# A two-block network on one core: inverse roots of the second block as powers on GpSimd, low parts of its weights and the delta rule's gating on VectorE

## The chip, the core and the metric

The kernel runs on one core of one Trainium2 chip. Its time is that of one execution in device microseconds; three executions of the kernel before were timed, and one more was taken with the hardware profiler. TensorE is called PE, VectorE DVE, ScalarE ACT, GpSimd POOL, as the profile calls them; SP is the engine that issues most DMAs.

## The reference, cut to what matters

A sequence of 256 positions of width 1024 passes two transformer blocks in float32. The change touches the second one only, from its mixer on. What it computes there, cut down:

```
h    = rms_norm(x, norm_mix)
qkv, z, a_g, b_g, c_q, c_kv, k_idx, w_idx, ug = split(h @ w_in)
# gated delta rule, 4 heads of 128, on silu(conv4(qkv))
q, k = q * rsqrt(sum(q*q) + eps), k * rsqrt(sum(k*k) + eps)
o    = delta_rule(q, k, v, decay, beta)
y_a  = o * rsqrt(mean(o*o) + eps) * gdn_norm * silu(z)
# attention over the 64 best keys of an index score; q and k are rms-normed
y_b  = sparse_attention(rms_norm(c_q @ w_qb), rms_norm(k of c_kv), v of c_kv, index score)
# convolution of 31 taps, then layer norm and silu
y_c  = silu(layer_norm(conv31(u * sigmoid(gate))))
x    = x + concat(y_a, y_b, y_c) @ w_out
x    = x + cross_attention(rms_norm(x), memory)     # q and k rms-normed per head of 128
x    = x + square(relu(rms_norm(x) @ w1)) @ w2
```

## The kernel before

A float32 matrix product is made of three products of numbers in a reduced format (`fp32r`): a matrix is split into a high part and a low part, and high x high, low x high and high x low are summed in PSUM (`mm3`, lines L232 to L234, and `add_T`, L395 to L397). Activations lie transposed, eight tiles of 128 channels by 256 positions, as `thi` and `tlo`. Weights come by DMA in pieces of 128 x 1024 (`load_w`): `wr` is the raw piece, ACT copies it to `wh` (L220 or L227), and the low part `wl` is `wr - wh`. By a share that `give` sets for each stage, `load_w` hands that subtraction either to POOL in one piece (L228) or to DVE in two halves (L222):

```
self.due += self.share
pool = self.due >= 1
```

In the second block's mixer (`block2_mix`, share `G2`) every fourth weight goes to POOL, in the cross attention (`block2_xa`, share `GX`) four of five, in the last feed-forward (`mlp`, share `GP`) none.

The mixer interleaves its parts by generators: `gdn_decay` and `tri_inverse` (the decay matrices `gam`, the key products `nqs`, and a triangular inverse in six doubling levels of two matrix products, a transpose and an addition, L1382 to L1389 and L1367) and then `gdn` lead; `fill2` fills in between with the remaining projections (`rest2`, matmuls into `fl`), the sparse attention (`dsa`) and the convolution of 31 taps on DVE (`conv31`, `cv_y`, L1514), at the end `conv_norm` and the first half of the output projection (`add_T`). A program then orders the instructions of each engine before the kernel runs; each engine executes its own list in that order and waits, in order, on semaphores. The lists are those shown below. `conv_silu` writes the four-tap convolutions `kq` and `vT`: ACT writes the first tap (L1070), DVE adds three (L1072).

Inverse roots are of two kinds. `rms_pow` sends a power of -0.5 to POOL as one instruction (L284). `rsqrt` computes a first guess from the bits and two Newton steps in seven (one column) or nine small instructions on DVE (L250 to L260). The second block calls `rsqrt` for `dsk` and `dsq` (keys and queries of the sparse attention, 2 and 8 columns), `gdr` twice (lengths of the delta rule's keys and queries, 8 columns), `rms` twice in `conv_norm`, `gdo` for each of the two chunks in `gdn` (4 columns), `xaq` twice in `block2_xa` (4 columns) and `raw` in `mlp`.

At the end of `gdn`, for each chunk of 128 positions, ACT sums the squares of the four heads, POOL multiplies the output by `silu(z)` (L1341), DVE multiplies by the root (L1343), and PE transposes the product (L1346) for the second half of the output projection. In the cross attention the row maxima `nm` are scaled by the root `xaq_y` (L892) before ACT's exponential.

Of the kernel before, what the change touches and what calls it, by code (L numbers as in the profile page):

```python
# [8 lines left out]
F32 = mybir.dt.float32  # L9
# [4 lines left out]
ALU = mybir.AluOpType  # L14
AX = mybir.AxisListType
PSUM = bass.MemoryType.PSUM

FW0 = 1
R1, R2, DS, CV, CK, CV0, NW, FW, WARM, WARM2, G1, GM, GF, G2, GX, GP = 2.0, 2.5, 3, 0.5, 1, 0.25, 24, 14, 7, 4, 0.05, 0.2, 0, 0.25, 0.8, 0
T = dict(bp=0, bq='gpsimd', xq='scalar', cp=3, w=(2,3,7,8), n=32, hold=1)  # L20
P = 128
SCRATCH = 4096
S = 256
D = 1024
NEG = -1.0e30
EPS = 1e-6
GDN_SCALE = 128 ** -0.5
# [90 lines left out]
class Net:  # L118
    def __init__(self, ctx, tc, ins, out, dumps=None):
        self.tc, self.nc, self.i, self.out = tc, tc.nc, ins, out  # L120
        self.dumps = dumps or {}
        pool = lambda n, b=1, **k: ctx.enter_context(tc.tile_pool(name=n, bufs=b, **k))
        self.cp = pool("cp")
        self.wp = pool("wp", 4)
        self.ap = pool("ap")
        self.sp = pool("sp", 2)
        self.pp = pool("pp", 4, space=PSUM)
        self.dp = pool("dp", 1, space=bass.MemoryType.DRAM)
        self.n = 0
        self.con = self.gate = None  # L130

    def give(self, share):

# [22 lines left out]
    def constants(self):  # L156
        nc = self.nc
        self.con = self.cp.tile([P, NCON], F32, tag="con", name="con")
        self.col = self.cp.tile([P, NCOL], F32, tag="col", name="col")
        self.srow = self.cp.tile([P, NSROW], F32, tag="srow", name="srow")  # L160
        n = CON["upper"]
        nc.scalar.dma_start(self.con[:, :n], self.i["const"][:, :n])
        n = COL["mix_norm_pre"] + NCH
        nc.scalar.dma_start(self.col[:, :n], self.i["cols"][:, :n])
        self.ident = self.con[:, CON["ident"]:CON["ident"] + P]
        self.upper = self.con[:, CON["upper"]:CON["upper"] + P]
        self.ones = self.cp.tile([P, P], F32, tag="ones", name="ones")
        nc.gpsimd.memset(self.ones, 1.0)
        self.mhalf = self.cp.tile([P, 1], F32, tag="mhalf", name="mhalf")
        nc.gpsimd.memset(self.mhalf, -0.5)  # L170
        self.zero = self.cp.tile([1, 512], BF16, tag="zero", name="zero")
        nc.gpsimd.memset(self.zero, 0.0)
        nc.scalar.activation(self.zero[:, 0:1], self.zero[:, 1:2], AF.Square)
# [68 lines left out]
    def rsqrt(self, v, shape, tag, bufs=2):  # L242


        nc = self.nc
        steps = (-0.703952253, 1.6819141), (-0.5, 1.5000004)
        y = self.t(shape, tag + "_y", bufs=bufs)
        t = self.t(shape, tag + "_t", bufs=bufs)
        h = [self.t(shape, tag + f"_h{k}", bufs=bufs) for k in range(2)]
        nc.vector.tensor_scalar(y.bitcast(I32), v.bitcast(I32), -0.5, 1595932665.0, op0=ALU.mult, op1=ALU.add)  # L250
        for k in range(2):
            nc.vector.tensor_scalar(h[k], v, steps[k][0], None, op0=ALU.mult)
        for k in range(2):
            if shape[1:] == [1]:
                nc.vector.tensor_scalar(t, y, y, h[k], op0=ALU.mult, op1=ALU.mult)
                nc.vector.tensor_scalar(y, t, steps[k][1], y, op0=ALU.add, op1=ALU.mult)
            else:
                nc.vector.tensor_tensor(t, y, y, op=ALU.mult)
                nc.vector.tensor_tensor(t, t, h[k], op=ALU.mult)
                nc.vector.scalar_tensor_tensor(y, t, steps[k][1], y, op0=ALU.add, op1=ALU.mult)  # L260
        return y
# [17 lines left out]
    def rms_pow(self, ss):  # L279

        v = self.t([P, 1], "rms_v", bufs=4)
        self.nc.vector.tensor_reduce(out=v, in_=ss, axis=AX.X, op=ALU.add)
        y = self.t([P, 1], "rms_y", bufs=4)
        self.nc.gpsimd.tensor_tensor(y, v, self.mhalf, op=ALU.pow)  # L284
        return y

    def new_T(self, place=None):
# [1005 lines left out]
    def gdn(self, kq, z, mixT):  # L1293
        nc = self.nc
        H = 4
        edec, ld, dd, kn, gam, nqs, room = self.gd
        inv, os, ws = room[:, 0], room[:, 1], room[:, 2]
        b4 = lambda c: c.unsqueeze(2).to_broadcast([P, H, P])
        v3 = lambda p: p.rearrange("p (h t) -> p h t", h=H)
        rqs, rhs, kd = self.side  # L1300
        state = None
        for i in range(2):
            tsl = slice(i * P, (i + 1) * P)
            if i:
                pks, pqs = self.ps(), self.ps()
                for h in range(H):
                    nc.tensor.matmul(pks[:, h * P:(h + 1) * P], kq[:, h, 0, tsl], state[:, h, :], start=True, stop=True)
                for h in range(H):
                    nc.tensor.matmul(pqs[:, h * P:(h + 1) * P], kq[:, h, 1, tsl], state[:, h, :], start=True, stop=True)
                ks = self.t([P, H, P], "gd_kd", bufs=1)  # L1310
                qs = os[:, 1]
                nc.vector.tensor_tensor(ks, v3(pks), b4(edec[:, i, :]), op=ALU.mult)
                nc.vector.tensor_tensor(rhs[:, i], rhs[:, i], ks, op=ALU.subtract)
                nc.vector.tensor_tensor(qs, v3(pqs), b4(edec[:, i, :]), op=ALU.mult)
            pw = self.ps()
            for h in range(H):
                nc.tensor.matmul(pw[:, h * P:(h + 1) * P], inv[:, i, h, :], rhs[:, i, h, :], start=True, stop=True)
            w = ws[:, i]
            nc.scalar.activation(w.rearrange("p h t -> p (h t)"), pw, AF.Copy)
            if i == 0:  # L1320
                pst = self.ps()
                for h in range(H):
                    nc.tensor.matmul(pst[:, h * P:(h + 1) * P], kd[:, h, :], w[:, h, :], start=True, stop=True)
                state = self.t([P, H, P], "gd_st", bufs=1)
                nc.scalar.activation(state.rearrange("p h t -> p (h t)"), pst, AF.Copy)
            po = self.ps()
            for h in range(H):
                nc.tensor.matmul(po[:, h * P:(h + 1) * P], nqs[:, i, h, 1, :], w[:, h, :], start=True, stop=True)
            o = os[:, i]
            if i:  # L1330
                nc.vector.tensor_tensor(o, v3(po), o, op=ALU.add)
                nc.vector.tensor_tensor(o, o, b4(rqs[:, i, :]), op=ALU.mult)
            else:
                nc.vector.tensor_tensor(o, v3(po), b4(rqs[:, i, :]), op=ALU.mult)
            yield

            sv = self.t([P, H], "gd_sv")
            for h in range(H):
                self.square_sum(o[:, h, :], sv[:, h:h + 1])
            nc.vector.tensor_scalar(sv, sv, 1.0 / P, EPS, op0=ALU.mult, op1=ALU.add)  # L1340
            nc.gpsimd.tensor_tensor(o, o, v3(z[:, i, :]), op=ALU.mult)  # L1341
            ro = self.rsqrt(sv, [P, H], "gdo")
            nc.vector.tensor_tensor(o, o, b4(ro), op=ALU.mult)  # L1343
            pt = self.ps()
            for h in range(H):
                nc.tensor.transpose(pt[:, h * P:(h + 1) * P], o[:, h, :], self.ident)  # L1346
            hi, lo = (m[:, 0:4, tsl] for m in mixT)
            gn = self.c("gdn_norm")
            nc.scalar.activation(hi, v3(pt), AF.Copy, scale=gn)
            nc.vector.scalar_tensor_tensor(lo, v3(pt), gn, hi.bitcast(F32), op0=ALU.mult, op1=ALU.subtract)  # L1350
            yield
# [219 lines left out]
    def block2_xa(self, xT, hT, ssx):  # L1571
        nc = self.nc
        kT, v = self.kv2
# [11 lines left out]
        def heads(j, tag):  # L1585
# [4 lines left out]
                    c = 2 * i + e  # L1590
                    nc.tensor.matmul(pss[:, c:c + 1], qT[:, 4 + 2 * j + e, i * P:(i + 1) * P], self.ones[:, 0:1], start=True, stop=True)
            for i in range(2):
                nc.vector.tensor_scalar(sv[:, i, :], pss[:, 2 * i:2 * i + 2], 1.0 / P, ve[:, i:i + 1], op0=ALU.mult, op1=ALU.add)
            rq = self.rsqrt(sv, [P, 2, 2], "xaq")
            nc.vector.tensor_scalar(rq, rq, GDN_SCALE, None, op0=ALU.mult)
            return [self.softmax_mem(i, 2 * j, score, v, P, oT, scale=rq[:, i, :], tag=tag) for i in range(2)]

        evac(self.chunk_T((0, 1), hT, "xa_wq", "cc", early=True), 0, 2)
        ve = self.t([P, 2], "xa_ve", bufs=1)
        nc.vector.tensor_scalar(ve, self.raw_sums(ssx), EPS / D, None, op0=ALU.mult)  # L1600
        evac(self.chunk_T((2,), hT, "xa_wq", "fl")[:, :S], 2, 1)
        units = heads(0, "cc")
        for u in units:
# [27 lines left out]
    def build(self, stages=99):  # L1631
# [11 lines left out]
        if stages <= 3:  # L1643
            return x
        self.give(G2)
        x = self.block2_mix(x)
        self.give(GX)
        x = self.block2_xa(*x)
# [151 lines left out]
```

## Time and profile before

| | us |
|---|---|
| median of 3 timed executions | 887.61 (885.38 to 888.46) |
| the profiled execution | 883.6 |
| its span from first to last instruction | 881.8 |
| PE busy, share of the span | 841.6 (95%) |
| DVE | 621.6 (70%) |
| ACT | 463.3 (53%) |
| POOL | 116.7 (13%) |
| mean granted clock of PE | 0.982 |

An engine is busy while an instruction of it is in flight; on PE ends are modelled, so a busy PE is not one at its peak. The granted clock is the share of PE's full clock that the chip allowed in a stretch. The first block, including the preparation of the second one's memory keys, lasts until about 465 us, the mixer from there to 655, the cross attention to 695, and the last feed-forward to the end.

### The profile page before, as it was taken

How to read it: one execution, taken by the hardware profiler on the slowest of the kernel's cores; microseconds unless marked ns; L12 is line 12 of the kernel's file. 1: busy time of each engine (PE TensorE's matmuls, PEld its weight loads, DVE VectorE, ACT ScalarE, POOL GpSimd, SP SyncE). 2: the span in 40 equal slices, each digit the busy share in tenths (PEclk: the TensorE clock that was granted, in tenths of full speed). 3: DMA queues.
4: the chain of work that ended last, by engine and by line, in shares of the span. 5: the costliest groups of instructions: out<-in, count | busy, mean ns of one | idle time of the engine just before them, and what ended most of it. 6: DMA issues, size and time to landing. Idle time of an engine off the chain costs nothing.

```text
span 881.8 us, 15073 instructions
## 1 busy us (share of the span) xinstructions
PE 841.6 (95%) x5725; PEld 764.2 (87%) x5725; DVE 621.6 (70%) x1394; ACT 463.3 (53%) x805; POOL 116.7 (13%) x125
## 2 busy tenths in 40 slices
PE   8899999998999999999999997899899999999998
PEld 6898887797879999999978987888797999999996
DVE  5579765656567788777776798997756776666663
ACT  5355554555556566655556564657455544444442
POOL 1224101212020000000011331621233000000000
PEclk9999999999999999999999997999989999999999
DMA  8984314567253667656633452202243365565551
GB/s 258 294 286 165 116 56 131 180 195 256 83 183 119 195 213 232 209 185 189 190 99 118 170 168 72 72 1 96 64 126 99 96 200 185 189 191 190 181 183 68
DMA packets 41012, 138.94 MB, mean 158 GB/s; under 512 B 4851, under 2 KB 6292, under 8 KB 40940
## 3 DMA queue, kind: packets, MB, share of 16 engines
q1 hardware_dynamic: 37440, 130.49, 46.1%
q10 hardware_dynamic: 2988, 6.06, 2.3%
q0 software_dynamic: 512, 1.44, 0.9%
q8 instruction: 45, 0.74, 0.3%
q14 instruction: 27, 0.22, 0.1%
HBM read 136.00 MB, written 1.44 MB: 156 GB/s over the span
## 4 chain that ended last, share of the span: by engine, by line
PE 75%; DVE 15%; ACT 4%; DMA 2%; issue 2%; POOL 1%; ACTq 0%; POOLq 0%; DVEq 0%; SPq 0%
PE tp L233 9%; PE tp L232 9%; PE tp L234 9%; PE fl L232 6%; PE fl L233 6%; PE fl L234 6%; PE cc L234 5%; PE cc L233 5%; PE cc L232 5%; DVE wl L222 3%; DVE cv_y L1514 3%; PE tp L914 1%; PE cc L746 1%; PE tp L724 1%; DVE kq L1072 1%
## 5 line engine op out<-in xcount | busy, mean ns | idle before, releaser
L222 DVE TENSOR_TENSOR wl<-wr,wh 128x512 fp32r<-128x512 f32 (+2 forms) x418 | 281.9, 699 | 116.1 <-ACT wh L220 114.2
L220 ACT ACTIVATE wh<-wr 128x1024 fp32r<-128x1024 f32 (+2 forms) x209 | 217.8, 1044 | 190.9 <-PE tp L233 80.7
L232 PE MATMUL tp<-thi,wh 128*128 128x256 f32 x784 | 222.1, 284 | 2.1 <-ACT wh L220 2.1
L234 PE MATMUL tp<-thi,wl 128*128 128x256 f32 x784 | 222.0, 283 | 0.2 <-DVE wl L222 0.2
L233 PE MATMUL tp<-tlo,wh 128*128 128x256 f32 x784 | 221.8, 283 | 0.0
L232 PEld LDWEIGHTS tp<-thi,wh 128*128 128x128 f32 x784 | 149.8, 191 | 3.7 <-ACT wh L220 2.3
L233 PEld LDWEIGHTS tp<-tlo,wh 128*128 128x128 f32 x784 | 149.8, 191 | 1.3
L234 PEld LDWEIGHTS tp<-thi,wl 128*128 128x128 f32 x784 | 149.8, 191 | 0.4 <-DVE wl L222 0.4
L228 POOL TENSOR_TENSOR wl<-wr,wh 128x1024 fp32r<-128x1024 f32 (+2 forms) x21 | 49.8, 2377 | 297.6 <-ACT wh L227 294.5
L227 ACT ACTIVATE ff_h<-ff_y 128x256 fp32r<-128x256 f32 x54 | 22.2, 416 | 43.8 <-PE fl L234 42.1
L232 PE MATMUL fl<-thi,wh 128*128 128x256 f32 x144 | 42.8, 297 | 1.7 <-ACT wh L220 1.0
L232 PE MATMUL cc<-wh,ff_h 128*128 128x512 f32 x108 | 42.4, 392 | 0.9 <-ACT ff_h L227 0.9
L234 PE MATMUL cc<-wh,ff_h 128*128 128x512 f32 x108 | 42.4, 393 | 0.0
L968 DVE SCALAR_TENSOR_TENSOR ff_y<-tp,col,ff_y 128x255 f32<-128x255 f32 x88 | 41.9, 476 | 0.7 <-ACT ff_y L966 0.6
L234 PE MATMUL fl<-wh,ff_h 128*128 128x512 f32 x108 | 42.2, 391 | 0.0
L233 PE MATMUL cc<-wl,ff_h 128*128 128x512 f32 x108 | 42.2, 391 | 0.0
L233 PE MATMUL fl<-wl,ff_h 128*128 128x512 f32 x108 | 42.2, 391 | 0.0
L232 PE MATMUL fl<-wh,ff_h 128*128 128x512 f32 x108 | 42.1, 390 | 0.0
L233 PE MATMUL fl<-tlo,wh 128*128 128x256 f32 x144 | 42.1, 292 | 0.0
L234 PE MATMUL fl<-thi,wl 128*128 128x256 f32 x144 | 42.0, 291 | 0.0
L227 ACT ACTIVATE wh<-wr 128x1024 fp32r<-128x1024 f32 (+3 forms) x23 | 22.5, 983 | 26.8 <-PE cc L396 5.8
L228 DVE TENSOR_TENSOR ff_h<-ff_y,ff_h 128x256 fp32r<-128x256 f32 x54 | 22.5, 422 | 14.9 <-ACT ff_h L227 14.9
(518 smaller groups left out, 1798.5 us busy)
## 6 DMA issues: line engine op xcount, KB each, us to landing
wr<-in_mlp_w_dram SPq DMA_DIRECT2D x64, 512.0 KB, 3.6
wr<-in_w_up_dram SPq DMA_DIRECT2D x44, 512.0 KB, 4.2
wr<-in_w_in_dram SPq DMA_DIRECT2D x31, 512.0 KB, 3.7
wr<-in_w_down_dram SPq DMA_DIRECT2D x22, 512.0 KB, 4.3
wr<-in_w_out_dram SPq DMA_DIRECT2D x16, 512.0 KB, 3.7
grow<-in_rows_dram ACTq DMA_DIRECT2D x8, 512.0 KB, 5.4
wr<-in_w_mk_dram SPq DMA_DIRECT2D x8, 512.0 KB, 4.5
wr<-in_w_mv_dram SPq DMA_DIRECT2D x8, 512.0 KB, 3.6
```

The costliest lines, as they stand in the source:

```text
L220: nc.scalar.activation(hi, raw, AF.Copy)
L222: nc.vector.tensor_tensor(lo[:, q], raw[:, q], hi[:, q].bitcast(F32), op=ALU.subtract)
L227: nc.scalar.activation(hi, raw, AF.Copy)
L228: (eng or nc.vector).tensor_tensor(lo, raw, hi.bitcast(F32), op=ALU.subtract)
L232: nc.tensor.matmul(out, a[0], b[0], start=first, stop=False)
L233: nc.tensor.matmul(out, a[0], b[1], start=False, stop=False)
L234: nc.tensor.matmul(out, a[1], b[0], start=False, stop=last)
L724: nc.tensor.matmul(pc[:, :2 * ns], qT[:, j, tsl], kT[:, :, br, :ns], start=True, stop=True)
L746: nc.tensor.matmul(out[:, h * 64:(h + 1) * 64], pT[:, (e * (i + 1) + b) * P:(e * (i + 1) + b + 1) * P], vsw[b][:, vo:vo + 64], start=(b == ...
L914: nc.tensor.matmul(pc[:, o:o + P], v[b][:, c * P:(c + 1) * P], pT[:, (2 * e + b) * P:(2 * e + b + 1) * P], start=(b == 0), stop=(b == 1))
L968: nc.vector.scalar_tensor_tensor(y[:, e, k:], a[:, :S - k], self.c("conv_w", 44 * (2 - k) + c), y[:, e, k:], op0=ALU.mult, op1=ALU.add)
L1514: nc.vector.scalar_tensor_tensor(y[:, c, k:], yg[:, c, :S - k], self.c("conv_dw", 2 * (30 - k) + c), y[:, c, k:], op0=ALU.mult, op1=ALU.add)
```

## The change

`rsqrt` becomes one power instruction on POOL once `power` is set, which `build` does ahead of the second block's mixer. The exponent tile `mhalf` gets eight columns. The shares `G2` and `GX` are 0, so that every low part of the second block's weights is computed on DVE in two halves. In `gdn`, ACT sums the squares of two heads, DVE those of the other two, and DVE multiplies by `silu(z)`. In `heads` the factors 1/128 and 128 to the power of -0.5 are folded into the sum under the root, which saves the multiplication of `rq`.

```diff
-R1, R2, DS, CV, CK, CV0, NW, FW, WARM, WARM2, G1, GM, GF, G2, GX, GP = 2.0, 2.5, 3, 0.5, 1, 0.25, 24, 14, 7, 4, 0.05, 0.2, 0, 0.25, 0.8, 0
+R1, R2, DS, CV, CK, CV0, NW, FW, WARM, WARM2, G1, GM, GF, G2, GX, GP = 2.0, 2.5, 3, 0.5, 1, 0.25, 24, 14, 7, 4, 0.05, 0.2, 0, 0, 0, 0
...
+        self.power = False
...
-        self.mhalf = self.cp.tile([P, 1], F32, tag="mhalf", name="mhalf")
+        self.mhalf = self.cp.tile([P, 8], F32, tag="mhalf", name="mhalf")
...
         y = self.t(shape, tag + "_y", bufs=bufs)
+        if self.power:
+            f = lambda a: a if len(shape) == 2 else a.rearrange("p a b -> p (a b)")
+            nc.gpsimd.tensor_tensor(f(y), f(v), self.mhalf[:, :math.prod(shape[1:])], op=ALU.pow)
+            return y
...
             sv = self.t([P, H], "gd_sv")
-            for h in range(H):
+            for h in range(2):
                 self.square_sum(o[:, h, :], sv[:, h:h + 1])
+            sq = self.t([P, 2, P], "gd_sq")
+            nc.vector.tensor_tensor(sq, o[:, 2:], o[:, 2:], op=ALU.mult)
+            nc.vector.tensor_reduce(out=sv[:, 2:], in_=sq, axis=AX.X, op=ALU.add)
             nc.vector.tensor_scalar(sv, sv, 1.0 / P, EPS, op0=ALU.mult, op1=ALU.add)
-            nc.gpsimd.tensor_tensor(o, o, v3(z[:, i, :]), op=ALU.mult)
             ro = self.rsqrt(sv, [P, H], "gdo")
+            nc.vector.tensor_tensor(o, o, v3(z[:, i, :]), op=ALU.mult)
             nc.vector.tensor_tensor(o, o, b4(ro), op=ALU.mult)
...
-                nc.vector.tensor_scalar(sv[:, i, :], pss[:, 2 * i:2 * i + 2], 1.0 / P, ve[:, i:i + 1], op0=ALU.mult, op1=ALU.add)
+                nc.vector.tensor_scalar(sv[:, i, :], pss[:, 2 * i:2 * i + 2], ve[:, i:i + 1], None, op0=ALU.add)
             rq = self.rsqrt(sv, [P, 2, 2], "xaq")
-            nc.vector.tensor_scalar(rq, rq, GDN_SCALE, None, op0=ALU.mult)
...
-        nc.vector.tensor_scalar(ve, self.raw_sums(ssx), EPS / D, None, op0=ALU.mult)
+        nc.vector.tensor_scalar(ve, self.raw_sums(ssx), P * EPS / D, None, op0=ALU.mult)
...
         self.give(G2)
+        self.power = True
         x = self.block2_mix(x)
```

With other instructions, the program that orders each engine's list arrives at other lists. The first place is DVE just ahead of the second pair of key convolutions (`kq<-fl`, the first rows of `rest2`); `cv_y` are taps of the long convolution, with 256 minus the tap's number of columns, `wl` low parts, `t` here the decay matrix. Before:

```order
L1199 TENSOR_SCALAR t_1024_5695<-t_1024_5695 128x512
L1514 SCALAR_TENSOR_TENSOR cv_y_5385<-yg_5257,col,cv_y_5385 128x244
L1514 SCALAR_TENSOR_TENSOR cv_y_5385<-yg_5257,col,cv_y_5385 128x243 x2
L222 TENSOR_TENSOR wl_6078<-wr_6075,wh_6077 128x512 x2
L1514 SCALAR_TENSOR_TENSOR cv_y_5385<-yg_5257,col,cv_y_5385 128x242 x2
L1514 SCALAR_TENSOR_TENSOR cv_y_5385<-yg_5257,col,cv_y_5385 128x241 x2
L1514 SCALAR_TENSOR_TENSOR cv_y_5385<-yg_5257,col,cv_y_5385 128x240 x2
L1072 SCALAR_TENSOR_TENSOR kq_5386<-fl_5705,col,kq_5386 128x255
```

The same place of the changed kernel, whose lines stand five to eight further down in the file:

```order
L1204 TENSOR_SCALAR t_1024_5699<-t_1024_5699 128x512
L1522 SCALAR_TENSOR_TENSOR cv_y_5387<-yg_5258,col,cv_y_5387 128x247 x2
L1522 SCALAR_TENSOR_TENSOR cv_y_5387<-yg_5258,col,cv_y_5387 128x246 x2
L223 TENSOR_TENSOR wl_6050<-wr_6047,wh_6049 128x512 x2
L1522 SCALAR_TENSOR_TENSOR cv_y_5387<-yg_5258,col,cv_y_5387 128x245 x2
L1522 SCALAR_TENSOR_TENSOR cv_y_5387<-yg_5258,col,cv_y_5387 128x244 x2
L223 TENSOR_TENSOR wl_6081<-wr_6078,wh_6080 128x512
L1077 SCALAR_TENSOR_TENSOR kq_5388<-fl_5709,col,kq_5388 128x255
```

The last tap ahead of `kq<-fl` had 240 columns and now has 244: eight instructions of the convolution have moved behind this place.

The second place is DVE at the end of `gdn`, second chunk, from the product with the query lengths (`gdr_y`) to the product that PE transposes. Before:

```order
L1332 TENSOR_TENSOR t_1024_5695<-t_1024_5695,gdr_y_6440 128x512
L222 TENSOR_TENSOR wl_7156<-wr_7153,wh_7155 128x512 x2
L1340 TENSOR_SCALAR gd_sv_7017<-gd_sv_7017 128x4
L250 TENSOR_SCALAR gdo_y_7028<-gd_sv_7017 128x4
...
L258 TENSOR_TENSOR gdo_t_7029<-gdo_y_7028 128x4
L222 TENSOR_TENSOR wl_7193<-wr_7190,wh_7192 128x512
L259 TENSOR_TENSOR gdo_t_7029<-gdo_t_7029,gdo_h_1330_7031 128x4
L222 TENSOR_TENSOR wl_7193<-wr_7190,wh_7192 128x512
L260 SCALAR_TENSOR_TENSOR gdo_y_7028<-gdo_t_7029,gdo_y_7028 128x4
L1343 TENSOR_TENSOR t_1024_5695<-t_1024_5695,gdo_y_7028 128x512
```

Of the changed kernel (L1350 is the product with `z` that was POOL's):

```order
L1337 TENSOR_TENSOR t_1024_5699<-t_1024_5699,gdr_y_6413 128x512
L1346 TENSOR_TENSOR gd_sq_6955<-t_1024_5699 128x256
L1347 TENSOR_REDUCE gd_sv_6950<-gd_sq_6955 128x2
L223 TENSOR_TENSOR wl_7041<-wr_7038,wh_7040 128x512
L1348 TENSOR_SCALAR gd_sv_6950<-gd_sv_6950 128x4
L1350 TENSOR_TENSOR t_1024_5699<-t_1024_5699,z_5174 128x512
L223 TENSOR_TENSOR wl_7041<-wr_7038,wh_7040 128x512
L1351 TENSOR_TENSOR t_1024_5699<-t_1024_5699,gdo_y_6959 128x512
```

Nine Newton steps and two low halves have left this stretch; a square, a sum and a product have come.

The third place is DVE around the norm of the convolution (`sg_st` and `sg_mv` are its statistics, `sg_v` the normed rows, `rms_y` the root from POOL), in the changed kernel:

```order
L1537 BN_STATS sg_st_6802<-fl_6799 128x6
L223 TENSOR_TENSOR wl_7004<-wr_7001,wh_7003 128x512
L1539 BN_AGGR sg_mv_6804<-sg_st_6802 128x2
L223 TENSOR_TENSOR wl_7004<-wr_7001,wh_7003 128x512
L1541 TENSOR_SCALAR sg_var_6806<-sg_mv_6804 128x1
L1544 TENSOR_SCALAR sg_v_6810<-fl_6799,sg_mv_6804,rms_y_6808 128x256
L1339 TENSOR_TENSOR t_1024_5699<-tp_6753,gdr_y_6413 128x512
```

Between `sg_var` and `sg_v` stood seven small steps on DVE; now there is nothing, and `sg_v` follows the power on POOL.

## Rows read from the trace of the kernel before

**Rows 1.** The page: busy us (share of the span) and number of instructions.

```profile
PE 841.6 (95%) x5725; PEld 764.2 (87%) x5725; DVE 621.6 (70%) x1394; ACT 463.3 (53%) x805; POOL 116.7 (13%) x125
```

**Rows 2.** Windows: stretch, length, busy us by engine (instructions), granted clock, DMA share, GB/s.

```profile
489.00:529.00 40.00, 38.80 (x300) 36.87 (x298) 38.61 (x68) 21.35 (x31) 13.20 (x6) 1.00 0.49 159
529.00:539.00 10.00, 5.46 (x25) 5.47 (x26) 10.00 (x39) 4.55 (x12) 1.09 (x1) 0.50 0.31 105
539.00:609.00 70.00, 65.20 (x521) 60.74 (x519) 62.37 (x201) 39.22 (x72) 20.02 (x16) 1.00 0.16 54
622.00:645.00 23.00, 18.08 (x132) 17.14 (x132) 14.40 (x27) 7.72 (x15) 3.64 (x2) 0.85 0.32 92
660.00:680.00 20.00, 17.90 (x116) 15.44 (x114) 14.65 (x47) 10.47 (x20) 7.05 (x3) 0.91 0.39 119
...
638.20:644.90 6.70, 4.09 (x18) 3.72 (x19) 2.44 (x2) 0.69 (x1) 1.14 (x1) 0.50 0.45 150
```

**Rows 3.** Waits of PE, 489 to 700 us: total us, times, longest.

```profile
PE cc L1420 <- ACT ds_v L1422: 5.7, 1, 5.7
PE tp L1346 <- DVE t L1343: 4.1, 1, 4.1
PE tp L1367 <- DVE t L1389: 2.6, 2, 1.6
PE fl L1591 <- ACT big L1583: 1.2, 1, 1.2
```

**Rows 4.** Timeline of DVE: start us, us, then the instruction.

```profile
497.62 1.28 DVE L222 TENSOR_TENSOR wl<-wr,wh 128x512 fp32r<-128x512 f32 x2
498.83 3.02 DVE L1514 SCALAR_TENSOR_TENSOR cv_y<-yg,col,cv_y 128x252 f32<-128x252 f32 x2
...
522.59 1.23 DVE L1514 SCALAR_TENSOR_TENSOR cv_y<-yg,col,cv_y 128x244 f32<-128x244 f32 x3
...
524.95 5.29 DVE L1514 SCALAR_TENSOR_TENSOR cv_y<-yg,col,cv_y 128x242 f32<-128x242 f32 x6
530.17 0.47 DVE L1072 SCALAR_TENSOR_TENSOR kq<-fl,col,kq 128x255 f32<-128x255 f32 x1
```

**Rows 5.** Timeline of POOL.

```profile
497.74 3.44 POOL L228 TENSOR_TENSOR wl<-wr,wh 128x1024 fp32r<-128x1024 f32 x1 [5.89 <-ACT wh L227]
...
523.53 2.45 POOL L1201 TENSOR_TENSOR t<-t,con 128x512 f32<-128x512 f32 x1 [9.24 <-ACT t L1200]
525.94 2.52 POOL L228 TENSOR_TENSOR wl<-wr,wh 128x1024 fp32r<-128x1024 f32 x1
...
637.00 2.34 POOL L228 TENSOR_TENSOR wl<-wr,wh 128x1024 fp32r<-128x1024 f32 x1 [2.29 <-ACT wh L227]
```

**Rows 6.** Timeline of ACT, 522 to 536 us; in brackets the idle time before.

```profile
524.31 0.45 ACT L1070 ACTIVATE kq<-fl,col 128x256 f32<-128x256 f32 x1
...
532.21 0.47 ACT L1070 ACTIVATE kq<-fl,col 128x256 f32<-128x256 f32 x1 [6.47 <-DVE kq L1072]
```

**Rows 7.** Timeline of DVE, 631 to 642 us.

```profile
630.90 0.69 DVE L1332 TENSOR_TENSOR t<-t,gdr_y 128x512 f32<-128x512 f32 x1
...
633.57 1.16 DVE L250 TENSOR_SCALAR gdo_y<-gd_sv 128x4 int32<-128x4 int32 x1
...
637.02 2.86 DVE L1343 TENSOR_TENSOR t<-t,gdo_y 128x512 f32<-128x512 f32 x1
```

**Rows 8.** Timeline of DVE, 665 to 671.5 us.

```profile
665.65 0.23 DVE L250 TENSOR_SCALAR xaq_y<-xa_sv 128x4 int32<-128x4 int32 x1
665.80 2.42 DVE L252 TENSOR_SCALAR xaq_h<-xa_sv 128x4 f32<-128x4 f32 x2
...
670.45 0.23 DVE L892 TENSOR_TENSOR nm<-nm,xaq_y 128x2 f32<-128x2 f32 x2
```

**Rows 9.** Groups by line and form on POOL, 440 to 700 us: count, busy us, mean ns.

```profile
L228 POOL TENSOR_TENSOR wl<-wr,wh 128x1024 fp32r<-128x1024 f32 x14 | 34.5, 2472 | 67.9 <-ACT wh L227 67.9
L1379 POOL TENSOR_TENSOR ti_m<-bq,con 128x512 f32<-128x512 f32 x12 | 15.3, 1299 | 16.3 <-PE tp L1382 16.3
...
L284 POOL TENSOR_TENSOR rms_y<-rms_v,mhalf 128x1 f32<-128x1 f32 x4 | 2.4, 605 | 9.5 <-DVE rms_v L282 9.5
```

More of the change, by code (lines that the diff above doesn't have):

```diff
@@ L283, in rms_pow @@
         y = self.t([P, 1], "rms_y", bufs=4)
-        self.nc.gpsimd.tensor_tensor(y, v, self.mhalf, op=ALU.pow)
+        self.nc.gpsimd.tensor_tensor(y, v, self.mhalf[:, :1], op=ALU.pow)
         return y
```

## The prediction

> **What bounds it now.** I read the page first: TensorE (PE) has work in flight for 841.6 us, 95% of the span [rows 1]. So time can only come from where PE waits or runs slowly, and I looked for such places inside the second block, which is all that the change touches. [...] The list of what PE waited for names the ends [rows 3]: 5.7 us for ACT's copy `ds_v`, 4.1 for DVE's gated output (L1343), 2.6 in two pieces for the triangular inverse (L1389), 1.2 in the cross attention.
>
> Why is DVE late? The timeline of DVE shows instructions that last several times their usual time exactly while GpSimd (POOL) computes a low part. Two taps of the convolution, 0.87 us elsewhere, last 3.02 us from 498.83, and six take 5.29 us from 524.95 where three undisturbed ones take 1.23 (a step of 0.38, so six would be about 2.4) [rows 4]; POOL's low parts run from 497.74 for 3.44 us and from 525.94 for 2.52 [rows 5]. With two more stretches like these, of 1.4 and 2.1 us, the excess from 489 to 530 is 1.4 + 2.2 + 2.1 + 2.9 = 8.6 us. The lateness goes on from there: the tap `kq<-fl` starts on DVE only at 530.17 [rows 4]; ACT, which wrote the first half of that tile at 524.31, stands 6.47 us for it until 532.21 [rows 6]; `ds_v` is queued behind that on ACT, and PE, in order, stands behind `ds_v` with its filler matmuls queued after it.
>
> The same stretching stands behind the other two waits. DVE's L1343 lasts 2.86 us from 637.02, beside a POOL low part of 2.34 us from 637.00 [rows 5, 7]; the first Newton step of `gdo_y` lasts 1.16 us [rows 7], beside the 128x512 gating product that POOL does now. In the cross attention two Newton steps (`xaq_h`) last 2.42 us [rows 8].
>
> **The change, part by part.** *Low parts.* Fourteen full ones and one of 536 columns leave POOL, at 2.47 us each there [rows 9], and come to DVE as two halves. A pair lasts 1.28 us [rows 4], 1.2 us of DVE's time, since the next instruction starts 0.08 before its end. Eight full pairs fall in the mixer, six around the cross attention. From 489 to 530 DVE gets the four pairs that were POOL's there: 4.8 us for 8.6 us of stalls. The two orders also show eight taps of the convolution (0.38 each, 3.0 us) behind the first `kq<-fl` that stood ahead of it. So DVE could be there 8.6 - 4.8 + 3.0 = 6.8 us earlier; it is held at 524.8, when ACT's first half is there, which is 5.4 us before 530.17. Term 1: PE's wait of 5.7 us shrinks by 5.0 (between 3.0, if POOL's mask product of 2.45 us at 523.53, which stays [rows 5], again catches a tap, and 5.4). Term 2: without that standstill the 10 us at the lower level need not come; the 5.5 us of work in it would take 2.7 at the higher. I take 2.0 (0 to 2.7).
>
> *Inverse roots.* Each root loses nine dependent DVE steps of about 0.15 us (seven for one column) and becomes one POOL instruction. The nearest row is the same power on one column, 0.60 us [rows 9]. Eight columns lie between that and eight times it, 4.8 us; since a product of 512 columns takes 1.30 us on POOL [rows 9], columns are cheap there, and I take 0.9 us for eight and 0.75 for four. From 539 to 609 four roots, 36 steps, leave a DVE that is 62.4 of 70 us busy [rows 2]; taken at 0.08 us of its time each that is 2.9 us, against eight taps (3.0) and one more pair (1.2) that arrive. So DVE's load there stays as it is, what improves is the latency ahead of the triangular inverse. Term 3: of the PE waits in this stretch (the two of L1389 and some smaller ones, 4.8 us by the window) I take 1.5 off (from 4.8 off to 3 more).
>
> *The gating in the tail (622 to 645).* Now the second chunk's product `t<-t,gdr_y` ends at 631.6, and L1343 at 639.9 [rows 7]: 8.3 us in which ACT sums four squares, POOL multiplies by z, DVE does nine Newton steps, two low halves, and L1343 is stretched. Afterwards DVE has, in its new order, a square of 256 columns (0.4), a sum (0.35), a low half (0.6), the scale (0.15), the product with z (0.6), a low half (0.6), the product with the root (0.7): 3.4 us, and the power (0.75, and up to 2.4) lies beside the product with z and the low half, which are 1.2 us. That ends near 635.1, and PE, which now stands 4.1 us before it can go on at L1343's end [rows 3], has filler until about 635.9. Term 4: the 4.1 us wait goes, and half of the 0.8 us that PE then stands for ACT's copy: 4.5 (3.0 to 4.9). Term 5: the stretch at the lower level holds 4.1 us of PE work [rows 2], worth 2.0 at the higher; I take 2.0 (0 to 2.0).
>
> *Cross attention.* The chain from the first Newton step (665.65) to the scaled maxima (670.45) [rows 8] is 4.8 us; the power at 0.75 us ends before the two maxima reductions do, even if these start 1.2 us sooner. Added pairs find 5.3 us of DVE idle time [rows 2]. Term 6: half of PE's 2.1 us of waits and half of the 1.8 lost to the lower level, 2.0 (0 to 3.9). Dropping the two scalings of `rq` and the 536-column low part at the end of the first feed-forward gives at most 1 us; I take 0.3 (term 7).
>
> *What comes in.* Around the convolution's norm the new order has DVE stand, in order, for a power twice (`sg_v` behind `rms_y`), and PE has only some 9 us of work between the transposes of `cv_y` and those of `sg_v`. The DVE instructions between them add up to about the same. I take 3.0 us of new PE waits there (0 to 6).
>
> The sum: 5.0 + 2.0 + 1.5 + 4.5 + 2.0 + 2.0 + 0.3 - 3.0 = 14.3 us off the profiled execution's 883.6, so 869.3. The median of the timed runs is 4.0 us above that execution; 873.3 is my forecast for it. With every term at its good end and nothing new it would be 24.7 us off, 862.9 for the median; at the bad ends terms 1 and 4 give 6.0, term 3 costs 3.0 and the new waits 6.0, so 3.0 more: 890.6.
>
> [...] The row is DVE at 38.6 of 40 us from 489 to 529 [rows 2], and this change gives that engine seventeen microseconds more. [...]
>
> **Rivals.** *Slower: DVE stays as busy as it was and gets the pairs on top.* This needs the stalls to come back through what POOL keeps (twelve mask products of 1.3 us [rows 9] and the powers). Then DVE has in 489 to 609 six pairs more (7.2) and 36 steps fewer (2.9): 4.3 us later, and PE, with DVE full, waits for it: 888 by the profile, 892. It decides where the stalls that go are under 4.3 us; I counted 8.6 by 530 alone. Chance 0.08. *Half given back:* the first two waits close, but the convolution, moved back by eight taps, and the norm's two powers make PE wait 6 us and more elsewhere with a new stretch at the lower clock: 877 to 884. For it speaks that PE executes in an order fixed beforehand with little filler there. Chance 0.22. *The power goes by columns:* 4.8 us for eight and 2.4 for four, with DVE held meanwhile; (3 x 4.2 + 4 x 1.8) = 20 us more on POOL, half of it felt: 880 to 886. Against it speaks the cheap column of the product. Chance 0.05. *Nothing changes:* the 5.7 us wait is due to ACT's order, not to DVE, and the tail's gain is lost at the norm: 886 to 889. ACT's wait on `kq` [rows 6] speaks against it. Chance 0.05.
>
> **Numbers.** The forecast's case, 864 to 880, has 0.60. The measurement can tell about 0.3%, 2.7 us. Faster by more: the forecast's case, the half case and part of the third, 0.85; within: 0.07; slower by more: 0.08. The range that leaves out no more than 2 in 10 is 863 to 885.
>
> **What would show it.** Right: no DVE instruction of the second block stretched to 1.5 us and more; PE's wait for `ds_v` under 1.5 us and a granted clock of 1.00 from 520 to 545; no wait of PE for L1351 (the new gated product) over 1 us; the power of eight columns under 1.2 us on POOL. Wrong: DVE full with PE waiting for `wl`; PE waiting for `cv_y` or `sg_v` by several microseconds; powers of 2 us and more; DVE stretched beside the powers or the masks.

## The result: 874.35 us, 1.3% faster

The changed kernel takes 874.35 us (median of 4 executions, 873.27 to 878.08), the kernel before 887.29 in the same comparison: a ratio of 0.987 [0.984, 0.990]. The forecast was 873.3. The profiled execution is the slowest of the four, 878.1 us, so its start has to be set apart: by PE's 401st matmul, at 61.58 us before and 66.52 after, it is 4.9 us late, in instructions that the change leaves alone. I therefore compare the second block from the same matmul to the same matmul: from the 2901st (449.46 us before, 454.66 after) to the 4701st (712.77 and 707.55) the kernel before takes 263.3 us and the changed one 252.9, which is 10.4 less.

The page of the changed kernel, as in [rows 1]: POOL has 28 us less, and DVE, which took the low parts over, 6 us less too.

```profile
PE 842.9 (96%) x5725; PEld 768.1 (88%) x5725; DVE 615.7 (70%) x1333; ACT 459.9 (52%) x795; POOL 88.9 (10%) x119
```

Its windows, with the columns of [rows 2]; the first three are taken 5 us later than there, as this profile is that much later:

```profile
494.00:534.00 40.00, 40.00 (x315) 38.63 (x314) 38.62 (x84) 24.89 (x41) 2.58 (x3) 1.00 0.57 185
534.00:544.00 10.00, 8.17 (x40) 7.60 (x39) 5.18 (x17) 2.62 (x5) 4.46 (x4) 0.66 0.00 0
544.00:614.00 70.00, 64.99 (x512) 60.10 (x512) 66.63 (x186) 39.56 (x75) 18.80 (x15) 0.98 0.16 48
622.00:645.00 23.00, 21.69 (x167) 21.16 (x168) 14.39 (x25) 9.12 (x15) 1.94 (x2) 0.93 0.28 73
660.00:680.00 20.00, 18.70 (x141) 17.15 (x140) 13.53 (x39) 12.44 (x30) 2.01 (x2) 1.00 0.33 106
```

PE no longer stands in the first stretch, though DVE got four pairs there: without the stalls DVE is as busy as it was, 38.62 us in place of 38.61, and no longer late. In the ten us behind it DVE now has idle time and PE still runs below full clock, 0.66 in place of 0.50; that is the gap in the gain, and the list of PE's waits (489 to 700 us; total, times, longest) names what stands there:

```profile
PE tp L1375 <- DVE t L1397: 4.0, 4, 1.7
PE tp L1354 <- DVE sg_var L1541: 2.9, 1, 2.9
PE cc L1437 <- DVE ds_kn L1436: 1.8, 1, 1.8
...
PE tp L1354 <- DVE t L1351: 0.5, 1, 0.5
```

The 5.7 us for `ds_v` and the 4.1 us for the tail's gated product of [rows 3] are gone. New are 1.8 us for `ds_kn` and 2.9 us that the list puts to `sg_var`. The inverse's waits have grown from 2.6 to 4.0.

**The wait for ds_kn.** POOL's timeline, then DVE's, of the changed kernel:

```profile
523.79 1.09 POOL L1206 TENSOR_TENSOR t<-t,con 128x512 f32<-128x512 f32 x1 [30.48 <-ACT t L1205]
532.52 0.70 POOL L251 TENSOR_TENSOR dsk_y<-ds_ss,mhalf 128x2 f32<-128x2 f32 x1 [7.63 <-DVE ds_ss L1431]
533.18 1.09 POOL L1206 TENSOR_TENSOR t<-t,con 128x512 f32<-128x512 f32 x1
534.23 1.64 POOL L251 TENSOR_TENSOR gdr_y<-gd_ss,mhalf 128x8 f32<-128x8 f32 x1
```

```profile
523.23 2.20 DVE L223 TENSOR_TENSOR wl<-wr,wh 128x512 fp32r<-128x512 f32 x2
...
533.25 0.35 DVE L1436 TENSOR_SCALAR ds_kn<-cc,dsk_y 128x128 f32<-128x128 f32 x1 [0.21 <-POOL dsk_y L251]
535.91 0.17 DVE L1211 TENSOR_TENSOR gd_dd<-gdr_y 128x8 f32<-128x8 f32 x1 [2.30 <-POOL gdr_y L251]
...
536.45 0.34 DVE L1436 TENSOR_SCALAR ds_kn<-cc,dsk_y 128x128 f32<-128x128 f32 x1
```

Three POOL instructions stand in line: the power for `dsk_y`, a mask, the power for `gdr_y` (its input is ready at 532.7). DVE, in order, stands 2.30 us for `gdr_y`, and the second half of `ds_kn`, whose root has been there since 533.2, is queued behind. PE waits for that half, and 6.8 us at the lower clock, a granted 0.50, follow from 537.2. PE's own list is part of this, as the run with powers from the cross attention on shows below.

**The wait put to sg_var.** DVE's timeline (brackets: idle time before):

```profile
620.59 0.16 DVE L1348 TENSOR_SCALAR gd_sv<-gd_sv 128x4 f32<-128x4 f32 x1
...
621.98 0.69 DVE L1351 TENSOR_TENSOR t<-t,gdo_y 128x512 f32<-128x512 f32 x1 [0.91 <-POOL gdo_y L251]
622.59 0.15 DVE L1541 TENSOR_SCALAR sg_var<-sg_mv 128x1 f32<-128x1 f32 x1
```

PE's instruction transposes the first chunk's gated product (L1351), which ends at 622.67 and starts PE at 622.82; `sg_var` only lies behind it. What is late is a chain: squares, sum, power, product.

### The profile page after: what moved, and what is told of

The parts are those of the page before. It is cut to its first block, busy times and chain, and to the rows that moved or that the text cites. A ratio compares the mean times of both kernels' runs of the same rounds, so it can differ in the third digit from the quotient of the medians.

```text
span 876.3 us, 14992 instructions
## 1 busy us (share of the span) xinstructions
PE 842.9 (96%) x5725; PEld 768.1 (88%) x5725; DVE 615.7 (70%) x1333; ACT 459.9 (52%) x795; POOL 88.9 (10%) x119
## 4 chain that ended last, share of the span: by engine, by line
PE 79%; DVE 10%; DMA 4%; ACT 3%; issue 2%; POOL 2%; ACTq 0%; SPq 0%; POOLq 0%; DVEq 0%
PE tp L235 10%; PE tp L233 10%; PE tp L234 10%; PE fl L233 6%; PE fl L234 6%; PE fl L235 6%; PE cc L235 5%; PE cc L234 5%; PE cc L233 5%; DVE wl L223 2%; PE cc L751 1%; DVE cv_y L1522 1%; DMA srow<-in_srows_dram 1%; PE tp L729 1%; PE tp L919 1%
## 5 line engine op out<-in xcount | busy, mean ns | idle before, releaser
L223 DVE TENSOR_TENSOR wl<-wr,wh 128x512 fp32r<-128x512 f32 (+2 forms) x448 | 301.3, 698 | 118.7 <-ACT wh L221 116.7
L221 ACT ACTIVATE wh<-wr 128x1024 fp32r<-128x1024 f32 (+2 forms) x224 | 233.0, 1044 | 214.3 <-PE tp L234 80.7
L289 POOL TENSOR_TENSOR rms_y<-rms_v,mhalf 128x1 f32<-128x1 f32 x16 | 9.8, 614 | 268.4 <-DVE rms_v L287 268.4
L233 PEld LDWEIGHTS fl<-thi,wh 128*128 128x128 f32 x144 | 28.4, 197 | 2.1 <-ACT wh L221 1.6
```

The costliest lines, as they stand in the source:

```text
L221: nc.scalar.activation(hi, raw, AF.Copy)
L223: nc.vector.tensor_tensor(lo[:, q], raw[:, q], hi[:, q].bitcast(F32), op=ALU.subtract)
L233: nc.tensor.matmul(out, a[0], b[0], start=first, stop=False)
L289: self.nc.gpsimd.tensor_tensor(y, v, self.mhalf[:, :1], op=ALU.pow)
```

## The experiments

A is the prediction's theory: DVE was held up beside POOL's low parts, and their removal is the gain. Rivals: B, the powers; C, the gating; D, POOL's time as such, since masks queue behind low parts. The eight combinations of the three parts were all measured; ratios are to the kernel before in the same comparison, the last columns are the time gained on its profile in the mixer (2901st to 4201st matmul) and the cross attention (to the 4701st):

```
shares powers gating   median   ratio  95%               mixer   cross att.
  -      -      -                1
  x      -      -      876.20   0.9876 [0.9850, 0.9903]   11.1     0.3
  -      x      -      886.45   1.0010 [0.9989, 1.0031]   -0.5     1.8
  -      -      x      882.37   0.9964 [0.9946, 0.9982]    3.0     1.4
  x      x      -      873.51   0.9859 [0.9837, 0.9880]    9.1     3.1
  x      -      x      872.72   0.9842 [0.9819, 0.9865]   13.5     0.1
  -      x      x      884.30   0.9979 [0.9961, 0.9996]   -1.2     1.9
  x      x      x      874.77   0.9867 [0.9845, 0.9889]    9.4     3.0   (first profile: 7.4, 3.1)
x  from cross a. x     870.78   0.9825 [0.9803, 0.9848]   13.6     3.1
```

**The changed kernel once more** (no edit).

> The changed kernel once more, to see what of a difference is the start of the execution alone. The two profiles differ by 4.9 us before PE's 400th matmul (61.6 us in the kernel before, 66.5 in the changed one), in instructions that the change leaves alone. If that is chance from one execution to the next, this profile has the 400th matmul anywhere between 61 and 67 us, the second block again takes about 253 us from matmul 2900 to matmul 4700 (263 before), and the median is 872 to 877. If it belongs to the change (other addresses, another program), the 400th matmul lies near 66.5 again.

874.77 us. The 401st matmul lies at 63.45, so the late start was chance: over all fourteen profiles of the study it lies between 60.5 and 66.6. The second block takes 250.8 us, 2.0 less than in the first profile, with 6.8 us at the lower clock where that had 13.7.

**Shares alone** (the lines of the power stand in this kernel too, switched off).

```diff
-... G2, GX, GP = ... 0.25, 0.8, 0
+... G2, GX, GP = ... 0, 0, 0
```

> The shares alone: all low parts of the second block on DVE, Newton steps and gating as before. Theory A (DVE was held up beside POOL's low parts, and that is most of the gain): 876 to 880, 8 to 11 us under the kernel before. Rival B (the powers are the gain; 17 us more on a full DVE cost time): 887 to 893. Rival C (the gating in the tail is the gain): 884 to 888.

876.20, as A has it; B and C are out as the main cause. Its window, and two of PE's waits:

```profile
529.00:539.00 10.00, 9.76 (x81) 9.15 (x79) 9.50 (x38) 6.05 (x14) 1.12 (x1) 1.00 0.27 105
```

```profile
PE tp L1351 <- DVE t L1348: 3.7, 2, 2.9
...
PE cc L910 <- DVE pr L905: 2.5, 1, 2.5
```

The stretch from 529 to 539 is whole: full clock, PE 9.76 of 10 us. The tail's wait (here L1351) stays, and so does one in the cross attention, so the other two parts have something to do there.

**The low parts put back, unread.**

```diff
+                g = self.wp.tile([P, 1024], R32, tag="ghost", ..., bufs=1)[:, :width]
+                nc.gpsimd.tensor_tensor(g, raw, hi.bitcast(F32), op=ALU.subtract)
...
-        self.give(G2)
+        self.give(G2, 0.25)
...
-        self.give(GX)
+        self.give(GX, 0.8)
```

> The changed kernel with the order of every engine as it is, and POOL, beside DVE, computes the same 15 low parts as in the kernel before once more into a tile that nobody reads. Theory A: DVE is held up again beside them, 2 us at a time, and as DVE has the pairs as well the time goes back to 882 to 890. If the gain came from the powers, the gating or the order: 874 to 876, as these stay.

897.0 (892.6 to 899.9), a ratio of 1.0113 [1.0085, 1.0141]: 22 us over the changed kernel, more than A expected, with every engine's order as it was. DVE's timeline, then POOL's:

```profile
492.53 4.11 DVE L224 TENSOR_TENSOR wl<-wr,wh 128x512 fp32r<-128x512 f32 x3 [2.49 <-ACT wh L222]
...
652.11 0.68 DVE L1142 COPY x<-cc 128x512 f32<-128x512 f32 x1
652.71 5.11 DVE L224 TENSOR_TENSOR wl<-wr,wh 128x512 fp32r<-128x512 f32 x2
```

```profile
492.58 2.92 POOL L229 TENSOR_TENSOR ghost<-wr,wh 128x1024 fp32r<-128x1024 f32 x1 [0.36 <-ACT wh L222]
...
648.72 5.74 POOL L229 TENSOR_TENSOR ghost<-wr,wh 128x1024 fp32r<-128x1024 f32 x2 [6.55 <-ACT wh L222]
654.74 2.53 POOL L229 TENSOR_TENSOR ghost<-wr,wh 128x1024 fp32r<-128x1024 f32 x1 [0.28 <-POOL ghost L229]
```

Three halves that take 1.9 us undisturbed take 4.11. Each time but one, a DVE instruction starts beside POOL's and lasts until 0.3 to 0.6 us after it (the one time only reductions out of PSUM run there); held against the same DVE instructions of the changed kernel, one by one, this adds 0 to 2.2 us at each of the fifteen, 27 us in sum. PE's waits show the old one, under its old name, and a new one:

```profile
PE cc L1434 <- ACT ds_v L1436: 5.8, 1, 5.8
PE tp L443 <- DVE ds_y L440: 5.5, 1, 5.5
```

**The control: POOL as busy, with powers.**

```diff
-                nc.gpsimd.tensor_tensor(g, raw, hi.bitcast(F32), op=ALU.subtract)
+                for _ in range(2):
+                    nc.gpsimd.tensor_tensor(g, self.ones[:, :8], hi[:, :8].bitcast(F32), op=ALU.pow)
```

> The control to the run with the extra low parts: in the same 15 places POOL computes two powers of eight columns, about 3.3 us, which no one reads. Theory A says that it is what the low parts read and write beside DVE that costs, not POOL's time: 874 to 877, and no DVE instruction lasts longer beside them. Rival D (what costs is that masks and powers queue behind a busy POOL): as much as with the extra low parts, 880 and more.

878.66, 3.9 over the changed kernel, a little above A's bound and far under the 22. POOL has 53.8 us of unread powers (the unread low parts were 37), and DVE's instructions beside them keep their length; POOL's row, then DVE's:

```profile
488.94 3.86 POOL L230 TENSOR_TENSOR ghost<-ones,wh 128x8 f32<-128x8 f32 x2 [0.36 <-ACT wh L222]
```

```profile
490.12 0.68 DVE L224 TENSOR_TENSOR wl<-wr,wh 128x512 fp32r<-128x512 f32 x1
...
491.31 0.68 DVE L224 TENSOR_TENSOR wl<-wr,wh 128x512 fp32r<-128x512 f32 x1
```

The 3.9 us are rival D, which is true in a small way: the mixer gains 7.2 us, as much as in the changed kernel's first profile, but the cross attention loses 3.7 where that gains 3.1. There POOL works on unread powers without a pause and `xaq_y` has to queue; DVE stands 5.0 us for it, and PE 3.7 us for DVE's copy `big` (L1593) queued behind. By the medians some 18 of the 22 us belong to what POOL's low parts do to DVE. By the profiles it is less: from the 2901st to the 4701st matmul the control takes 259.9 us and the run with unread low parts 274.2, so 14 us between them, since the control's profile is 2.0 us quicker from the 1401st to the 2901st matmul, in work that the edit leaves alone; why is open.

**Powers alone, gating alone, both** (as in the change's diff, on the kernel before; the line that switches the powers on, without the gating's lines or with them).

```diff
+        self.power = True
         x = self.block2_mix(x)
```

> The powers alone (with the factors folded in the cross attention): low parts shared with POOL and gating as before. Theory A (DVE held up beside POOL's low parts is most of the gain): 882 to 888, since all fifteen low parts stay on POOL, and powers queue behind them; the stretched DVE instructions of 2 to 3 us are all there. Rival B (the powers are a gain of their own size): 876 to 880.

> The gating on VectorE alone: shares and Newton steps as before. Theory A: 883 to 889; the wait of PE for the gated product in the tail shrinks from 4.1 to under 3 us only if no low part of POOL falls beside it, the wait of 5.7 us for ds_v stays. Rival C (the gating in the tail is a gain by itself): 880 to 883.

> Powers and gating, low parts shared with POOL as before. Theory A, that the shares carry the change: 881 to 886, with PE's wait for ds_v of 5.7 us still there. If powers and gating together carry half of it: 876 to 880.

886.45, 882.37 and 884.30: no change to be told, a small gain, and a smaller one. The first and the last are as A has it; the second lies just under A's range and in C's, so the gating is a gain of its own, of about 3 us. In all three PE still waits 5.7 us for `ds_v`. With the powers alone the triangular inverse's wait is longer: DVE is late there, with four low halves of 1.31 to 2.65 us from 553 to 562 us beside POOL's masks and a low part; of this run's waits (before: 2.6, longest 1.6):

```profile
PE cc L1425 <- ACT ds_v L1427: 5.7, 1, 5.7
PE tp L1372 <- DVE t L1394: 5.1, 2, 4.5
```

**Shares with one other part.** The same lines with the shares at 0.

> Shares and powers, gating as before. By the single edits so far (shares -10, powers +1, gating -3 us against the kernel before) a plain sum is 876 to 878. If the powers in the mixer cost about 4 us once the stalls are gone (the run with powers only from the cross attention on was 4 us faster than the changed kernel), and give back 2.7 in the cross attention: 876 to 879, with the old wait for the gated product in the tail. If powers and shares help each other (POOL being free for them): 870 to 874.

> Shares and gating, Newton steps everywhere. A plain sum of the single edits is 872 to 874. If the powers help in the cross attention and cost in the mixer: the mixer takes as long as in the run with powers from the cross attention on (13.6 us under before), the cross attention gains under 1 us instead of 3.1, and the time is 872 to 875. If powers help in the mixer too: 877 and more.

Shares with powers take 873.51, which is the case that the two help each other; they do, but in the cross attention only (0.3 to 3.1), while the mixer loses 2.0. Shares with gating take 872.72, as expected if powers cost in the mixer. Over the eight, the mean ratio with the shares is 0.9861, without them 0.9988: 11 us. The powers make +0.7 us (0.9929 against 0.9921), the gating -2.1 us (0.9913 against 0.9936). Once the shares are in, the powers cost 2.0 us and more in the mixer (11.1 to 9.1, 13.5 to 9.4 or 7.4) and give 2.8 to 2.9 in the cross attention.

**Powers from the cross attention on.**

```diff
-        self.power = True
         x = self.block2_mix(x)
         self.give(GX)
+        self.power = True
```

> The changed kernel with Newton steps on DVE in the mixer, powers from the cross attention on. The run with the shares alone took 11.0 us off the mixer (to matmul 4200) where the changed kernel takes 7.4 and 9.4 off in two profiles, but gained 0.3 in the cross attention where it gains 3.0. If the mixer's powers cost (the wait for sg_v of 2.9 us, new at the norm), and gating takes the 3.7 us of waits in the tail that the shares alone leave: 868 to 872. If the difference in the mixer is the chance of one order against another: 873 to 877.

870.78, the lowest median of the study (that of shares with gating, 872.72, lies within its interval), about 4 us under the changed one; the two intervals, of separate comparisons, just meet at 0.9845 to 0.9848. Its window and the longest of its waits:

```profile
529.00:539.00 10.00, 9.76 (x83) 9.47 (x82) 9.49 (x38) 5.54 (x14) 1.12 (x1) 1.00 0.32 105
```

```profile
PE tp L1375 <- DVE t L1397: 2.6, 3, 1.4
PE fl L1548 <- DVE gdo_y L265: 2.1, 1, 2.1
```

The wait of 1.8 us for `ds_kn` is down to 0.2, and the clock stays full there. The Newton steps are not quicker than the powers. PE's two instructions on `ds_kn` in the changed kernel:

```profile
534.03 0.27 PE L1437 MATMUL cc<-con,ds_kn 128*128 128x128 f32 x1
536.85 0.33 PE L1437 MATMUL cc<-con,ds_kn 128*128 128x128 f32 x1 [1.83 <-DVE ds_kn L1436]
```

In this run, DVE's second half, then PE:

```profile
537.15 0.35 DVE L1436 TENSOR_SCALAR ds_kn<-cc,dsk_y 128x128 f32<-128x128 f32 x1
```

```profile
536.78 0.33 PE L1437 MATMUL cc<-con,ds_kn 128*128 128x128 f32 x1 [0.24 <-DVE ds_kn L1436]
537.66 0.27 PE L1437 MATMUL cc<-con,ds_kn 128*128 128x128 f32 x1
```

With Newton steps the second half is ready at 537.50, with powers at 536.79, and PE passes the 3401st matmul at 527.15 and 527.31. But PE's first instruction on `ds_kn` is its 3471st with Newton steps and its 3450th with powers, in every profiled run with shares at 0: the program that orders the lists put 21 matmuls fewer ahead of it. So the powers bring the operand sooner, and the list asks for it sooner still. That the program counted on a shorter power is likely, but not shown.

**Newton steps at the convolution's norm only.**

```diff
-        if self.power:
+        if self.power and shape != [P, 1]:
```

> The changed kernel with Newton steps for the two roots of one column in the convolution's norm, all other powers kept. If PE's wait of 2.9 us for the rows behind the norm's power is the price of putting that power between two DVE instructions: the wait falls under 1 us and the time is 870 to 873. If DVE is late there for its own work: the wait stays, 874 to 877.

The first case is a miss and the second one holds: 874.61, and the wait is the same to a tenth, in the list of PE's waits of this run:

```profile
PE tp L1354 <- DVE sg_var L1541: 2.9, 1, 2.9
```

The norm's two powers cost nothing that the times can tell; the wait belongs to the gated product.

**The masks on DVE too** (edit of the kernel with powers from the cross attention on).

```diff
-            nc.gpsimd.tensor_tensor(m, nqs[:, i, :, 0, :], lev(0), op=ALU.mult)
+            nc.vector.tensor_tensor(m, nqs[:, i, :, 0, :], lev(0), op=ALU.mult)
...
-                nc.gpsimd.tensor_tensor(m, nqs[:, i, :, 0, :], lev(k), op=ALU.mult)
+                nc.vector.tensor_tensor(m, nqs[:, i, :, 0, :], lev(k), op=ALU.mult)
```

> The kernel with powers only from the cross attention on, and the fourteen mask products of the triangular inverse (ti_m) on DVE too. They still stretch DVE instructions, by some 7 us by the rows of that run. If that is worth more than the 14 products of about 0.6 us that DVE gets (8.4 us), or the shorter step in the chain of the inverse (1.1 to 1.5 us on POOL) counts: 867 to 870. If DVE, full from 539 to 609 us, only trades stalls for work: 870 to 873. If DVE becomes the bound there: 874 and more.

875.41, 4.6 slower than without the edit, the third case by its time. What DVE loses beside POOL in the mixer falls from about 5 to 1.8 us (the 7 us expected counted instructions beside two masks twice), but the fourteen masks bring some 8.4 us of work to an engine that was 67.3 of 70 us busy. The mixer gains 7.9 us in place of 13.6; 5.2 of the difference arise from the 4001st to the 4201st matmul, where PE runs 6.8 us at the lower clock in place of 3.4. What makes DVE late there was not followed up; the new wait of PE in that part is this:

```profile
PE tp L1354 <- DVE rms_y L261: 4.1, 1, 4.1
```

## Why the prediction was right, and which of its terms were not

**The cause was right.** The shares are 11 of the 12 to 13 us, and a low part on POOL costs what was read from [rows 4, 5]: put back unread, they bring the stalls and the wait for `ds_v` back. The first rival (DVE gets the pairs on top while the stalls stay, 892) is what that run builds; it came to 897. In the comparison of the experiments the kernel before, with fifteen low parts on POOL, took 886.4 us, and the shares alone, with all of them on DVE, took 876.2.

**The terms.** By the count of matmuls (the orders differ, so to about 1 us), two profiles of the changed kernel:

| term | predicted | changed kernel | shares alone |
|---|---|---|---|
| 1 and 2, `ds_v` and the clock behind it | 7.0 | 3.3, 4.9 | 8.2 |
| 3, the inverse, to the 4001st matmul | 1.5 | -0.2, 0.5 | 0.8 |
| 4, 5 and the new waits, to the 4201st | 3.5 | 3.2, 3.0 | 1.0 |
| 6, cross attention | 2.0 | 3.1, 3.0 | 0.3 |
| 7, the 536-column low part | 0.3 | 1.1, 1.1 | 1.1 |
| sum | 14.3 | 10.4, 12.5 | 11.4 |

Terms 2, 5 and 6 reckon with half the speed where the granted clock is 0.50 [rows 2]. PE's timeline of the changed kernel has matmuls on 256 columns start every 0.21 us at 0.50 (538.78 to 540.48) and every 0.12 at 1.00 (649.79 to 651.95), a factor of 1.8.

Terms 1 and 2 were right for the shares and lost 3 to 5 us to a step that I mis-sized: the powers in the mixer. The row of POOL's groups, 440 to 720 us:

```profile
L251 POOL TENSOR_TENSOR gdr_y<-gd_ss,mhalf 128x8 f32<-128x8 f32 x2 | 3.3, 1640 | 8.2 <-DVE gd_ss L1239 8.2
L251 POOL TENSOR_TENSOR gdo_y<-gd_sv,mhalf 128x4 f32<-128x4 f32 x2 | 2.4, 1220 | 16.0 <-DVE gd_sv L1348 16.0
...
L251 POOL TENSOR_TENSOR rms_y<-sg_var,mhalf 128x1 f32<-128x1 f32 x2 | 1.1, 556 | 26.6 <-DVE sg_var L1541 26.6
```

Eight columns take 1.64 us where I took 0.9, four 1.01 to 1.39 where I took 0.75: with the 0.56 us of one column, each further column adds about 0.15 us in the mean, far more than a product's (1.30 us for 512 columns [rows 9]). The rival by which the power goes by columns had that much right, though 1.64 us are far from its 4.8 and no DVE instruction is held meanwhile. And I counted the power's length only, not the queue ahead of it on POOL and behind it on DVE, which made the 2.30 us of idle DVE, nor PE's list, which asks for `ds_kn` 21 matmuls earlier than with Newton steps. "What improves is the latency ahead of the triangular inverse" came true in small (its first mask starts at 543.04 us, at 543.88 with Newton steps in the run with powers from the cross attention on), but term 3 did not follow from it: the inverse's own waits grew to 4.0 us where that run has 2.6. Why was not followed up.

**New waits: right in size, wrong in place.** The 3.0 us at the norm came as 2.9 us, but for the first chunk's gated product, and Newton steps at the norm leave it. Of the signs named, `ds_v` is gone as said, but the granted clock from 534 to 544 is 0.66, PE waits over 1 us for L1351, and a power of eight columns is above 1.2 us. DVE is stretched beside the masks (a low half of 1.58 us at 543.14, to be held against 0.68; a pair of 2.20 at 523.23, to be held against 1.28), not beside the powers.

**The tail** went as predicted in its sum: the shares alone leave 3.7 us of waits for the gated product, shares with gating and no mixer powers bring the mixer from 11.1 to 13.5 us. **The cross attention** gained 1 us more than predicted, and needs both parts: with the powers but not the shares it gains 1.8 or 1.9, with the shares but not the powers 0.1 or 0.3, with both 3.0 to 3.2. Part of this is where the lower clock falls. Gating alone, which changes nothing in that part, gains 1.4 us, and the 3.4 us at the lower clock that begin at 675.6 in the kernel before are absent there.

**The base** held: 4.0 us were added since the profile of before is a quick execution. At the 1401st matmul, the thirteen other profiles lie 3.4 us behind it in the middle (-0.4 to 5.5).

So the sum was 2 to 4 us too high against the profiles of the second block, and 1.4 to 2.6 against the medians (14.3 against 12.9, and 11.7 with the changed kernel once more). That it came so near is in part luck: terms 6 and 7 gave 1.8 us more than predicted, which hides as much of what terms 1 to 3 lack. What sets the 2 us between two profiles of the changed kernel is open: they differ in how long the lower clock lasts after a wait, 13.7 and 6.8 us in sum.

## What to carry to other kernels

Price work on GpSimd by what it does to VectorE, not by its own idle time: look for VectorE instructions that last until a GpSimd instruction ends (here three low halves took 4.11 us in place of 1.9 beside a low part of 2.92 us on GpSimd). When one change bundles several edits, measure them one by one; here one carried the gain, and another gave in one stage what it took in the other. A small function on another engine pays where its latency lies beside other work (the root beside the maxima, in the cross attention, where the powers gave 2.8 to 2.9 us), and can cost where the next instruction of an in-order engine waits for it (2.30 us of idle VectorE for `gdr_y`), or where another engine's list, fixed beforehand, asks for the result too early (`ds_kn`, 21 matmuls earlier).

## What the runs showed of the hardware that I had not expected

- Not every DVE instruction is held beside a long POOL instruction. In the run with unread low parts `x<-cc`, a copy out of PSUM, takes its usual 0.68 us at 652.11 while POOL is at work. The pairs of low halves around it, whose inputs both lie in SBUF, take 3.51 us from 648.68 and 5.11 from 652.71, where an undisturbed pair takes 1.28. Why the copy is spared was not shown.
- A step with one SBUF input was held too. In the kernel before, the first Newton step of `gdo_y`, which reads 4 columns of one tile, takes 1.16 us from 633.57 [rows 7] and ends some 0.02 us after this one:

```profile
633.41 1.30 POOL L1341 TENSOR_TENSOR t<-t,z 128x512 f32<-128x512 f32 x1 [12.63 <-ACT junk L265]
```

  Undisturbed it takes about 0.16.
- Beside the powers it was otherwise. They read two SBUF operands on GpSimd, as the low parts do, and low halves beside 3.86 us of them last 0.68 us each, as undisturbed: none of the 30 unread powers on eight columns held a DVE instruction up (two of them had none beside them).
- A power's time on GpSimd rises with its columns, though not by them alone: in the changed kernel 0.56 us for one, 0.70 and 1.09 for two, 1.01 to 1.39 for four and 1.64 for eight; the unread ones, of eight, took 1.80 in the mean.
